# Folds, casts and sums moved off GpSimd in an inference step of a Fourier and latent-attention layer

## The chip, the cores and the metric

One core of a Trainium2 chip runs the kernel. The metric is device time in microseconds of one execution, as the median of several runs. The engines are TensorE (PE, with PEld for its weight loads), VectorE (DVE), ScalarE (ACT), GpSimd (POOL) and SyncE (SP), which issues most DMAs. The profile gives TensorE's granted clock as a fraction of 2.4 GHz; its two levels are 1.2 and 2.4 GHz.

## The reference

One trunk layer over 1024 latent tokens and 128 context tokens of width 1024 (1152 rows, written NT):

```
h      = rms_norm(x) * (1 + scale) + shift          # shift, scale, gate from silu(cond) @ w_ada
u_f, z_f, cq, ckv, k_rope, z_a, g_f, g_a = split(h @ w_in)
y_f    = (Re FFT2(u_f, positions x 128 channels) * silu(z_f)) @ w_f_out
attn   = softmax(q k) v      # 8 heads, low-rank q and kv, latents read 128 cached context rows too
y_a    = (attn * silu(z_a)) @ w_a_out
merged = sigmoid(g_f) * y_f + sigmoid(g_a) * y_a
y      = rms_norm(x + gate * (merged @ w_out)) * final_norm_g
```

Outputs are y for context and latent tokens, and the context's normalised ckv and k_rope.

## The kernel before, in words

All products are made in a rounded 32-bit format: an operand is split into a high part (a cast) and a low part (operand minus high part), and `mm3` (lines 122 to 126) issues three matmuls, high-high, low-high or high-low. So each operand costs a cast and a subtraction before TensorE can use it. `hi_pool` casts on GpSimd, `act.copy` on ScalarE, `lo_dve` (line 109) subtracts on VectorE.

The work falls into stages. (1) The first part, up to about 95 us: x is loaded, scaled and transposed by matmuls; for each of eight channel blocks f of 128 channels, `modulate` makes h (1024 latent columns and 128 context columns), `fold` and `fold2` add and subtract mirrored positions for the Fourier transform (sums s1, differences s2, quarter folds q0 and q1, context folds c2 and c3), `fsplit` makes the high and low parts foh and fol, `hsplit` those of h (hTh, hTl), and `mix` multiplies the folded rows with the channel-transformed weights into five PSUM banks. The steps stand in the list SEQ, an order written by hand: x, u, a are loads, Q R S the norm, T t transposes, c C the modulation's rows, m modulate, s fold, h hsplit, f fold2, g fsplit, w weights, X mix. The table ENG names the engine of each elementwise step: a ScalarE, d VectorE, p GpSimd. (2) A first plain block of w_in (`Plain`), the position transform, three low-rank maps (`low_mm`), a second plain block; meanwhile `combine` loads h again from DRAM and forms differences of its quarters. (3) From about 182 to 426 us, eleven pairs of blocks of w_in (`pair`): each pair is made with seven products in the order 1, 6, 2, 7, 5, 4, 3 in place of eight, from sums of quarter blocks. `Blocks.prepare` makes the weights' sums and splits for the next pair while the present one runs; product 1 lands in bank X, ScalarE copies it into a buffer u, and product 2 accumulates into the same bank. (4) The product with w_f_out and the low-rank rows' transposes, to about 500 us; (5) attention, to about 776 us; (6) the merge, to about 825 us: per block m and a third of the columns, `merge_part` multiplies by the gate, adds the Fourier branch, and splits the sum; (7) the output projection and the last norm.

Tiles of 4.6 KB per partition come from one pool of 43 (`U`); a tile is reused when its last reader is done, and the instruction that writes it next waits for that. Each engine works through its instructions in one fixed order. That order is found when the program is built, by a planner that starts from the order of the code and moves instructions by its own costs.

Of the kernel before, what the change touches and what calls it, by code (L numbers as in the profile page):

```python
# [12 lines left out]
AF = mybir.ActivationFunctionType  # L13
ALU = mybir.AluOpType
# [3 lines left out]
P = 128  # L18
# [21 lines left out]
).split()  # L40
GRP = ((8, 0, 1), (2, 3), (4, 5), (6, 7))
ENG = dict(c0="a", c1="a", c2="d", c3="p", s0="a", s1="d", s2="p", q0="p", q1="d", h0="a", l0="p", h1="a", l1="d", hh="a", hl="d", ma="a", mb="d", mc="d", md="a", ta="d", tb="a", tc="a", wh="a", ar="a")
SCE = "ddddddddd"


# [18 lines left out]
def kernel(ctx: ExitStack, tc: tile.TileContext, a: dict):  # L64
    nc = tc.nc
    pe, act, dve, pool = nc.tensor, nc.scalar, nc.vector, nc.gpsimd
# [19 lines left out]
    def U(shape, dt=F32, s="u"):  # L86
        return upool.tile(shape, dt, tag="u", name=nm(s))
# [4 lines left out]
    def S(shape, dt=F32, tag="s1k", bufs=3, s="s"):  # L92
        return spool.tile(shape, dt, tag=tag, bufs=bufs, name=nm(s))
# [7 lines left out]
    def MM(tag="mm"):  # L101
        tag = tag if tag in banks else "mm"
        return psum.tile([P, 512], F32, tag=tag, bufs=banks[tag], name=nm(tag))

    def hi_pool(out, x):
        pool.tensor_scalar(out=out, in0=x, scalar1=1.0, scalar2=1.0, op0=ALU.mult, op1=ALU.mult)  # L106

    def lo_dve(out, x, hi):
        dve.tensor_tensor(out=out, in0=x, in1=hi.bitcast(F32), op=ALU.subtract)  # L109
# [11 lines left out]
    def mm3(out, lh, ll, rh, rl, start, stop, after=False, on=False):  # L121
        i = pe.matmul(out, lh, rh, start=start, stop=False, skip_group_check=on)  # L122
        if after:
            tc.keep_in_program_order(i)
        pe.matmul(out, lh, rl, start=False, stop=False, skip_group_check=on)  # L125
        pe.matmul(out, ll, rh, start=False, stop=stop, skip_group_check=on)  # L126
# [47 lines left out]
    def load_x(t):  # L174
        x = U([P, D], s="x")
        src = a["x_sample"][t * P : (t + 1) * P, :] if t < 8 else a["x_prompt"]
        nc.sync.dma_start(x, src)
        return x
# [29 lines left out]
    def EQ(k, out, x):  # L208
        e = ENG[k]
        if e == "a":  # L210
            act.copy(out, x)
        elif e == "p":
            hi_pool(out, x)
        else:
            dve.tensor_copy(out, x)

    def TT(k, out, x, y, op):
        (pool if ENG[k] == "p" else dve).tensor_tensor(out=out, in0=x, in1=y, op=op)

# [8 lines left out]
    def ada_rows(parts, kper, n, ps):  # L228
# [10 lines left out]
        ada = S([P, n], tag="s1k", bufs=3) if n == 256 else U([P, n], s="ada")  # L239
        (act.copy if n == 512 or ENG['ar'] == 'a' else dve.tensor_copy)(ada, ps[:, 0:n])  # L240
        return ada
# [4 lines left out]
    def wprime(k):  # L246
# [9 lines left out]
        h = WPh[k // 2][:, k % 2, :].rearrange("p (c g) -> p c g", g=4)  # L256
        (act.copy if ENG["wh"] == "a" else dve.tensor_copy)(h, ps)
        lo_dve(WPl[k // 2][:, k % 2, :].rearrange("p (c g) -> p c g", g=4), ps, h)
# [22 lines left out]
    def modulate(f):  # L281
        hf = hfs[f] = U([P, NT], F32, "hf")
        if f < ND:
            pa, pb = xT.pop(f)
            src = ((0, hf[:, 0:512], pa, ENG["ma"] == "a"), (0, hf[:, 512:NL], pb, ENG["mb"] == "a"), (1, hf[:, NL:NT], xTc[:, f, :], ENG["mc"] == "a"))
        else:
            src = ((0, hf[:, 0:NL], xT.pop(f), ENG["md"] == "a"), (1, hf[:, NL:NT], xTc[:, f, :], ENG["mc"] == "a"))
        for m, out, x, e in src:
# [6 lines left out]
    def fold(f):  # L295
        hf = hfs[f]

        sd = U([P, 2, 513], F32, "sd")
        EQ("s0", sd[:, 0, 0:513:512], hf[:, 0:513:512])
        TT("s1", sd[:, 0, 1:512], hf[:, 1:512], hf[:, 1023:512:-1], ALU.add)  # L300
        TT("s2", sd[:, 1, 1:512], hf[:, 1:512], hf[:, 1023:512:-1], ALU.subtract)
        pool.tensor_scalar(out=sd[:, 1, 0:513:512], in0=sd[:, 1, 256:257].to_broadcast([P, 2]), scalar1=0.5, scalar2=1.0, op0=ALU.mult, op1=ALU.mult)

        fo = fos[f] = U([P, 1153], F32, "fo")
        EQ("c0", fo[:, 1024:1025], sd[:, 0, 256:257])
        EQ("c1", fo[:, 1025:1090:64], hf[:, 1024:1089:64])
        TT("c2", fo[:, 1026:1089], hf[:, 1025:1088], hf[:, 1151:1088:-1], ALU.add)
        TT("c3", fo[:, 1090:1153], hf[:, 1025:1088], hf[:, 1151:1088:-1], ALU.subtract)
        sds[f] = sd
# [236 lines left out]
    def combine(f):  # L546
        xa, xb = U([P, NT], F32, "xa"), U([P, NT], F32, "xb")
        nc.sync.dma_start(xa, h_d[f])
        nc.sync.dma_start(xb, h_d[f + 4])
        x11, x12, x21, x22 = xa[:, lo_half], xa[:, hi_half], xb[:, lo_half], xb[:, hi_half]  # L550
        dve.tensor_tensor(out=x11, in0=x12, in1=x11, op=ALU.subtract)
        pool.tensor_tensor(out=x12, in0=x22, in1=x12, op=ALU.subtract)
        dve.tensor_tensor(out=x22, in0=x22, in1=x11, op=ALU.subtract)
        dve.tensor_tensor(out=x21, in0=x21, in1=x22, op=ALU.subtract)
        h, l = U([P, NT], F32R, "th"), U([P, NT], F32R, "tl")
        act.copy(h, xb)
        lo_dve(l, xb, h)
        t42.append((h, l))
        if f % 2 == 0:
            t33.append((U([P, NT], F32R, "th"), U([P, NT], F32R, "tl")))  # L560
        sl = hi_half if f % 2 else lo_half
        h, l = (x[:, sl] for x in t33[f // 2])
        act.copy(h, x12)
        lo_dve(l, x12, h)
        ones.append(x11)
# [130 lines left out]
    class Blocks:  # L696
# [10 lines left out]
        def prepare(self, j):  # L707
            (a11, a12), (a21, a22) = [(r[:, 0], r[:, 1]) for r in self.raw]
            if j == 6:
                self.s12 = U([P, 2, 512], F32, "ws")  # L710
                pool.tensor_tensor(out=self.s12[:, 0], in0=a21, in1=a22, op=ALU.add)
                pool.tensor_tensor(out=self.s12[:, 1], in0=self.s12[:, 0], in1=a11, op=ALU.subtract)
            elif j == 7:
                self.s34 = U([P, 2, 512], F32, "ws")
                pool.tensor_tensor(out=self.s34[:, 0], in0=a11, in1=a21, op=ALU.subtract)
            elif j == 3:
                pool.tensor_tensor(out=self.s34[:, 1], in0=a12, in1=self.s12[:, 1], op=ALU.subtract)
            x = {1: lambda: a11, 2: lambda: a12, 3: lambda: self.s34[:, 1], 4: lambda: a22, 5: lambda: self.s12[:, 0],
                 6: lambda: self.s12[:, 1], 7: lambda: self.s34[:, 0]}[j]()
            w = U([P, 2, 512], F32R, "wp")  # L720
            hi_pool(w[:, 0], x)
            lo_dve(w[:, 1], x, w[:, 0])
            self.w[j] = w

# [89 lines left out]
    for p in range(2):  # L814
        fourier_out(p)
    combine(0)
    low_out(0, pss)
    pss = low_mm(1)
    combine(1)
    low_out(1, pss)  # L820
    pss = low_mm(2)
    combine(2)
    low_out(2, pss)
    pss = None
# [169 lines left out]
    def q_chunk(wq, c):  # L994
        sl = slice(c * CH, (c + 1) * CH)
        ps = MM()
        for k in range(2):
            ws = slice(k * P, (k + 1) * P)
            mm3(ps[:, :CH], wq[:, 0, ws], wq[:, 1, ws], cqh[k][:, sl], cql[k][:, sl], k == 0, k == 1)
        qf = H([P, CH], s="qf")  # L1000
        dve.tensor_tensor(out=qf, in0=ps[:, :CH], in1=TAB[:, sl], op=ALU.mult)  # L1001
        q = U([P, 2, CH], F32R, "q")
        hi_pool(q[:, 0, :], qf)
        lo_pool(q[:, 1, :], qf, q[:, 0, :])
        return q
# [18 lines left out]
    for m in range(8):  # L1024
# [10 lines left out]
        mf = U([P, NT], F32, "mf")  # L1035
        for c in range(3):
            sl = slice(c * CH, (c + 1) * CH)
# [177 lines left out]
    for h in range(NH):  # L1215
# [3 lines left out]
        q0 = None  # L1219
        for part in LSEQ if h == NH - 1 else HSEQ:  # L1220
# [46 lines left out]
            elif o == "Q":  # L1267
# [3 lines left out]
                elif h + 1 < NH:  # L1271
                    q0 = q_chunk(wq1, 0)
# [12 lines left out]
    def merge_part(m, c):  # L1285
        w, ga, mf = wao[m]
        sl = slice(c * CH, (c + 1) * CH)
        ps = MM()
        for k in range(4):
            mm3(ps[:, :CH], w[:, 0, k, :], w[:, 1, k, :], ath[k][:, sl], atl[k][:, sl], k == 0, k == 3)  # L1290
        dve.tensor_tensor(out=ga[:, sl], in0=ps[:, :CH], in1=ga[:, sl], op=ALU.mult)
        pool.tensor_tensor(out=mf[:, sl], in0=mf[:, sl], in1=ga[:, sl], op=ALU.add)  # L1292
        act.copy(mh[m][:, sl], mf[:, sl])
        lo_dve(ml[m][:, sl], mf[:, sl], mh[m][:, sl])

# [13 lines left out]
    for m, c in ((0, 0), (0, 1), (1, 0), (1, 1), (0, 2), (1, 2)):  # L1309
        merge_part(m, c)  # L1310
    load_out(0)
    load_out(1)
    for m in range(2, 8):
        merge_open(m)
        for c in range(3):
            merge_part(m, c)
        load_out(m)
# [7 lines left out]
    for t in range(9):  # L1325
        x = load_x(t)
        g = gate[0 if t < 8 else 1]
        sl = slice(t * P, (t + 1) * P)
# [4 lines left out]
        for i, (c0, c1) in enumerate(zip(cuts, cuts[1:])):  # L1333
            ps = MM()
            hf, n = c0 // 512, c1 - c0
            for k in range(8):
                wh, wl = wo[hf, k // 2]
# [168 lines left out]
```

## Time and profile before

| quantity | value |
|---|---|
| median of 3 runs | 935.27 us (933.52 to 939.51) |
| the profiled execution: its time, its span | 937.2 us, 935.4 us |
| busy: PE, PEld, DVE, ACT, POOL | 898.3, 849.3, 620.7, 424.2, 404.8 us |
| mean granted clock | 0.990 |
| first matmul of the first plain block | 94.81 us |
| DMA | 115.61 MB, mean 124 GB/s |

The span runs from the first to the last instruction. A busy engine may still be slow, since matmuls' ends are modelled and overlap; the share of an average hides stages with different limits, so the windows are read stage by stage.

### The profile page before, as it was taken

The numbers are of one execution on the slowest core, as the hardware profiler recorded it, in microseconds if no ns is written. First come the engines' busy times: TensorE is split into PE (matmuls) and PEld (weight loads), VectorE is DVE, ScalarE is ACT, GpSimd is POOL, SyncE is SP. The second block draws the span as 40 slices with busy tenths as digits, with TensorE's granted clock in tenths as the row PEclk, the third lists the DMA queues.
The fourth block names the chain that finished last, engine by engine and source line by source line (L and its number), as shares of the span: only waits on it lengthen the run. The fifth ranks groups of instructions, "written<-read, shape, count | busy, mean of one in ns | idle before, by whom it ended". The sixth has DMA issues, their size and how long they took to land.

```text
span 935.4 us, 15960 instructions
## 1 busy us (share of the span) xinstructions
PE 898.3 (96%) x5886; PEld 849.3 (91%) x5886; DVE 620.7 (66%) x1257; ACT 424.2 (45%) x1171; POOL 404.8 (43%) x491
## 2 busy tenths in 40 slices
PE   4988999999999999999999999999999999999996
PEld 3878999999999999988899999999999989988885
DVE  2789456664555545648538889889889888884333
ACT  6555365411122111135227787787787782212111
POOL 0378313574444448932151264264263126863221
PEclk9988999999999999999999999999999999999998
DMA  9733745422223244287743000000000147342222
GB/s 363 313 140 104 230 140 204 159 96 97 96 96 97 96 147 146 96 280 290 264 149 136 6 7 5 7 7 4 7 7 1 63 152 296 122 158 90 90 92 89
DMA packets 35798, 115.61 MB, mean 124 GB/s; under 512 B 4484, under 2 KB 9348, under 8 KB 35720
## 3 DMA queue, kind: packets, MB, share of 16 engines
q1 hardware_dynamic: 31688, 105.94, 31.5%
q10 hardware_dynamic: 3168, 6.16, 1.8%
q0 software_dynamic: 864, 2.49, 0.8%
q8 instruction: 47, 0.77, 0.3%
q14 instruction: 31, 0.25, 0.1%
HBM read 81.74 MB, written 32.83 MB: 122 GB/s over the span
## 4 chain that ended last, share of the span: by engine, by line
PE 75%; POOL 5%; DVE 3%; DMA 3%; ACT 1%; issue 1%; DVEq 0%; SPq 0%; ACTq 0%; POOLq 0%
PE mm L122 20%; PE mm L126 20%; PE mm L125 20%; PE mm L1128 6%; PE mm L1149 4%; PE mm L1148 3%; POOL z L758 1%; POOL wp L106 1%; DMA za_d<-z 1%; POOL z L762 1%; DMA fz_d<-z 1%; DVE tl L109 1%; DMA wr<-in_w_f_out 1%; POOL mfl L1292 1%; DVE hTl L109 0%
## 5 line engine op out<-in xcount | busy, mean ns | idle before, releaser
L1096 DVE TENSOR_REDUCE s<-mm 128x1 f32<-128x384 f32 (+1 forms) x200 | 104.7, 540 | 15.6 <-PE mm L126 13.8
L109 DVE TENSOR_TENSOR tl<-mm,th 128x384 fp32r<-128x384 f32 (+1 forms) x216 | 102.9, 505 | 16.7 <-ACT th L1129 16.1
L1107 ACT ACTIVATE p<-mm,s 128x384 f32<-128x384 f32 x192 | 110.1, 588 | 7.1 <-DVE s L1101 6.8
L122 PE MATMUL mm<-hTh,wp 128*128 128x288 f32 x352 | 103.8, 296 | 1.9 <-ACT u L789 1.9
L125 PE MATMUL mm<-hTl,wp 128*128 128x288 f32 x352 | 103.7, 295 | 0.0
L126 PE MATMUL mm<-hTh,wp 128*128 128x288 f32 x352 | 103.7, 295 | 0.0
L1129 ACT CAST th<-mm 128x384 fp32r<-128x384 f32 (+1 forms) x216 | 89.5, 461 | 25.4 <-PE mm L1128 22.4
L1128 PE MATMUL mm<-c,p 128*128 128x128 f32 x576 | 95.5, 273 | 1.6 <-DVE tl L109 0.5
L1128 PEld LDWEIGHTS mm<-c,p 128*128 128x128 f32 x576 | 71.6, 140 | 8.4 <-DVE tl L109 1.4
L125 PE MATMUL mm<-tl,wp 128*128 128x288 f32 x264 | 77.8, 295 | 1.4 <-DVE tl L109 1.4
L122 PE MATMUL mm<-th,wp 128*128 128x288 f32 x264 | 78.1, 297 | 0.2 <-DVE u L795 0.2
L126 PE MATMUL mm<-th,wp 128*128 128x288 f32 x264 | 77.9, 295 | 0.0
L1149 PE MATMUL mm<-tl,v 128*128 128x384 f32 (+1 forms) x216 | 73.9, 346 | 0.2 <-DVE tl L109 0.2
L1148 PE MATMUL mm<-th,v 128*128 128x384 f32 (+1 forms) x216 | 73.3, 343 | 0.0
L122 PE MATMUL mm<-kh,q 128*128 128x384 f32 x192 | 70.8, 368 | 0.7 <-DVE osb L1162 0.4
L122 PEld LDWEIGHTS mm<-hTh,wp 128*128 128x128 f32 x352 | 66.2, 188 | 2.1 <-ACT u L789 2.1
L125 PEld LDWEIGHTS mm<-hTl,wp 128*128 128x128 f32 x352 | 66.2, 188 | 0.0
L126 PEld LDWEIGHTS mm<-hTh,wp 128*128 128x128 f32 x352 | 66.2, 188 | 0.0
L125 PE MATMUL mm<-kl,q 128*128 128x384 f32 x192 | 64.7, 337 | 0.0
L126 PE MATMUL mm<-kh,q 128*128 128x384 f32 x192 | 63.8, 337 | 0.0
L106 POOL TENSOR_SCALAR q<-qf 128x384 fp32r<-128x384 f32 x24 | 12.3, 512 | 105.5 <-DVE qf L1001 77.7
L122 PE MATMUL mm<-hi,mh 128*128 128x512 f32 (+1 forms) x152 | 57.5, 382 | 0.0
(341 smaller groups left out, 2581.6 us busy)
## 6 DMA issues: line engine op xcount, KB each, us to landing
wr<-in_w_in SPq DMA_DIRECT2D x24, 512.0 KB, 4.1
x<-in_x_sample SPq DMA_DIRECT2D x16, 512.0 KB, 4.9
wada<-in_w_ada SPq DMA_DIRECT2D x16, 512.0 KB, 10.2
h_d<-hf SPq DMA_DIRECT2D x8, 576.0 KB, 3.0
gf_d<-z SPq DMA_DIRECT2D x8, 576.0 KB, 4.3
gfl<-gf_d SPq DMA_DIRECT2D x8, 576.0 KB, 5.1
mf_d<-mf SPq DMA_DIRECT2D x8, 576.0 KB, 3.6
gal<-ga_d SPq DMA_DIRECT2D x8, 576.0 KB, 3.7
```

Source lines behind the costliest of these rows:

```text
L106: pool.tensor_scalar(out=out, in0=x, scalar1=1.0, scalar2=1.0, op0=ALU.mult, op1=ALU.mult)
L109: dve.tensor_tensor(out=out, in0=x, in1=hi.bitcast(F32), op=ALU.subtract)
L122: i = pe.matmul(out, lh, rh, start=start, stop=False, skip_group_check=on)
L125: pe.matmul(out, lh, rl, start=False, stop=False, skip_group_check=on)
L126: pe.matmul(out, ll, rh, start=False, stop=stop, skip_group_check=on)
L758: pool.tensor_tensor(out=out, in0=out, in1=tmp, op=ALU.mult)
L1096: dve.tensor_reduce(out=self.nb if self.last else self.mx[:, kc : kc + 1], in_=ps[:, 0:n], axis=AX.X, op=ALU.min)
L1107: act.activation(self.p[:, kc * CH : kc * CH + n], self.ps[kc][:, 0:n], AF.Exp, scale=-1.0, bias=self.nb, accum_out=SSP[(self.h // 2) % 2] ...
L1128: pe.transpose(pt[:, j * P : (j + 1) * P], self.pr[j][:, kt * P : (kt + 1) * P], ident)
L1129: act.copy(th[:, i, 0:n], pt[:, 0:n])
L1148: pe.matmul(po[:, 0:n], V[kt][:, h, :], th[:, i, 0:n], start=(self.nv == 0), stop=False)
L1149: pe.matmul(po[:, 0:n], V[kt][:, h, :], tl[:, i, 0:n], start=False, stop=(self.nv == 8))
```

## The change

Eight steps change their engine; nothing else does. In the table ENG: the context's difference c3, the difference fold s2, the quarter folds q0 and the second low part l0 go from GpSimd to VectorE; the context's modulation mc and the copies ta of the transposes' first half go from VectorE to ScalarE. In `fold`, the scaling of two columns goes from GpSimd to ScalarE. In `combine`, one of four subtractions goes from GpSimd to VectorE; in `Blocks.prepare` the cast of each weight operand from GpSimd to ScalarE (its sums stay on GpSimd); in `merge_part` the addition from GpSimd to VectorE.

```diff
-ENG = dict(... c3="p", s0="a", s1="d", s2="p", q0="p", q1="d", h0="a", l0="p", ... mc="d", md="a", ta="d", ...)
+ENG = dict(... c3="d", s0="a", s1="d", s2="d", q0="d", q1="d", h0="a", l0="d", ... mc="a", md="a", ta="a", ...)
...
-        pool.tensor_scalar(out=sd[:, 1, 0:513:512], in0=sd[:, 1, 256:257].to_broadcast([P, 2]), scalar1=0.5, scalar2=1.0, op0=ALU.mult, op1=ALU.mult)
+        act.activation(sd[:, 1, 0:513:512], sd[:, 1, 256:257].to_broadcast([P, 2]), AF.Copy, scale=0.5)
...
-        pool.tensor_tensor(out=x12, in0=x22, in1=x12, op=ALU.subtract)
+        dve.tensor_tensor(out=x12, in0=x22, in1=x12, op=ALU.subtract)
...
-            hi_pool(w[:, 0], x)
+            act.copy(w[:, 0], x)
             lo_dve(w[:, 1], x, w[:, 0])
...
-        pool.tensor_tensor(out=mf[:, sl], in0=mf[:, sl], in1=ga[:, sl], op=ALU.add)
+        dve.tensor_tensor(out=mf[:, sl], in0=mf[:, sl], in1=ga[:, sl], op=ALU.add)
         act.copy(mh[m][:, sl], mf[:, sl])
```

## Rows read from the trace of the kernel before

**Rows 1.** Windows: stretch, its length, busy PE PEld DVE ACT POOL (instructions), clock, DMA.

```profile
40.00:96.00 56.00, 48.41 (x363) 43.55 (x360) 49.21 (x61) 32.26 (x59) 41.18 (x42) 0.88 0.35 120
...
182.00:402.00 220.00, 219.79 (x1657) 219.45 (x1656) 119.23 (x179) 41.37 (x97) 132.94 (x142) 1.00 0.30 107
...
776.00:840.00 64.00, 63.19 (x345) 60.59 (x345) 53.52 (x65) 12.70 (x25) 46.78 (x41) 1.00 0.51 184
...
60.00:68.00 8.00, 7.27 (x43) 6.30 (x41) 6.23 (x11) 5.28 (x10) 5.53 (x6) 0.57 0.25 101
```

**Rows 2.** Waits from 36 to 100 us: sum in us, times, longest.

```profile
ACT fo L211 <- DVE sd L218: 12.9, 7, 3.6
ACT fo L211 <- DVE hf L293: 5.9, 3, 3.4
...
PE mm L126 <- DVE fol L218: 2.5, 3, 1.1
```

**Rows 3.** VectorE's groups from 40 to 96 us: count, busy us, mean ns, idle before.

```profile
L218 DVE TENSOR_TENSOR fol<-fo,foh 128x641 fp32r<-128x641 f32 x8 | 13.1, 1647 | 2.3 <-ACT foh L211 2.3
L218 DVE TENSOR_TENSOR hTl<-hf,hTh 128x1152 fp32r<-128x1152 f32 x8 | 11.7, 1471 | 2.4 <-ACT hTh L211 2.3
L218 DVE TENSOR_TENSOR fo<-sd 128x512 f32<-128x512 f32 x7 | 9.1, 1303 | 1.2 <-POOL fo L218 1.2
L218 DVE TENSOR_TENSOR sd<-hf 128x511 f32<-128x511 f32 x6 | 4.5, 744 | 0.0
L293 DVE TENSOR_SCALAR hf<-xTc,c 128x128 f32<-128x128 f32 x6 | 4.3, 732 | 0.0
L109 DVE TENSOR_TENSOR wpl<-mm,wph 128x512 fp32r<-128x512 f32 x5 | 3.3, 684 | 1.5 <-ACT wph L257 1.5
L218 DVE TENSOR_TENSOR fo<-hf 128x63 f32<-128x63 f32 x6 | 2.3, 381 | 0.0
```

**Rows 4.** VectorE's time line where GpSimd is quiet: start, duration.

```profile
65.24 0.81 DVE L218 TENSOR_TENSOR fol<-fo,foh 128x641 fp32r<-128x641 f32 x1
...
66.14 0.21 DVE L218 TENSOR_TENSOR fo<-hf 128x63 f32<-128x63 f32 x1
66.28 0.68 DVE L218 TENSOR_TENSOR sd<-hf 128x511 f32<-128x511 f32 x1
...
87.61 1.34 DVE L218 TENSOR_TENSOR hTl<-hf,hTh 128x1152 fp32r<-128x1152 f32 x1
```

**Rows 5.** GpSimd's largest group from 40 to 92 us.

```profile
L218 POOL TENSOR_TENSOR fol<-fo,foh 128x512 fp32r<-128x512 f32 x8 | 12.3, 1548 | 3.4 <-ACT foh L211 3.3
```

**Rows 6.** ScalarE's cast of 512 columns, from 40 to 96 us.

```profile
L211 ACT CAST foh<-fo 128x512 fp32r<-128x512 f32 x7 | 4.3, 619 | 1.3 <-DVE fo L218 1.3
```

**Rows 7.** TensorE's time line at the start of the paired blocks.

```profile
181.23 0.40 PE L125 MATMUL mm<-tl,wp 128*128 128x288 f32 x1 [1.44 <-DVE tl L109]
```

**Rows 8.** GpSimd's casts and two of its sums, 182 to 402 us.

```profile
L106 POOL TENSOR_SCALAR wp<-ws 128x512 fp32r<-128x512 f32 x40 | 27.3, 683 | 17.2 <-PE mm L126 15.6 <-DVE wp L109 0.6
...
L717 POOL TENSOR_TENSOR ws<-wr,ws 128x512 f32<-128x512 f32 x10 | 17.0, 1701 | 0.0
...
L715 POOL TENSOR_TENSOR ws<-wr,wr 128x512 f32<-128x512 f32 x10 | 13.8, 1384 | 7.1 <-PE mm L126 6.5 <-DVE wp L109 0.6
```

**Rows 9.** Time lines of GpSimd, ScalarE and TensorE at the last pair's start.

```profile
399.91 2.02 POOL L758 TENSOR_TENSOR z<-z,u 128x288 f32<-128x288 f32 x2
...
399.92 0.45 ACT L756 ACTIVATE u<-z 128x288 f32<-128x288 f32 x1 [1.36 <-DVE z L775]
...
412.08 0.40 PE L122 MATMUL mm<-hTh,wp 128*128 128x288 f32 x1 [1.88 <-ACT u L789]
```

**Rows 10.** The merge, 762 to 840 us: two groups, then VectorE's time line.

```profile
L109 DVE TENSOR_TENSOR ml<-mfl,mh 128x384 fp32r<-128x384 f32 x24 | 20.1, 861 | 1.0 <-ACT mh L1293 1.0
...
L1292 POOL TENSOR_TENSOR mfl<-mfl,gal 128x384 f32<-128x384 f32 x24 | 29.8, 1255 | 13.5 <-DVE gal L1291 13.5
...
826.37 1.48 DVE L109 TENSOR_TENSOR ml<-mfl,mh 128x384 fp32r<-128x384 f32 x3
```

More of the change, by code (lines that the diff above doesn't have):

```diff
@@ L41 @@
 GRP = ((8, 0, 1), (2, 3), (4, 5), (6, 7))
-ENG = dict(c0="a", c1="a", c2="d", c3="p", s0="a", s1="d", s2="p", q0="p", q1="d", h0="a", l0="p", h1="a", l1="d", hh="a", hl="d", ma="a", mb="d", mc="d", md="a", ta="d", tb="a", tc="a", wh="a", ar="a")
+ENG = dict(c0="a", c1="a", c2="d", c3="d", s0="a", s1="d", s2="d", q0="d", q1="d", h0="a", l0="d", h1="a", l1="d", hh="a", hl="d", ma="a", mb="d", mc="a", md="a", ta="a", tb="a", tc="a", wh="a", ar="a")
 SCE = "ddddddddd"
```

## The prediction

> **What bounds the kernel now.** I read the table of windows first. TensorE is busy 219.8 of 220 us in the long stage of the paired blocks and 63.2 of 64 us in the merge, but only 48.4 of 56 us between 40 and 96 us, where the folds feed the mixing products; there VectorE is busy 49.2 us and GpSimd 41.2 us [rows 1]. In 60 to 68 us the granted clock is 0.57 on average, between the levels 1.2 and 2.4 GHz: some 6.9 of these 8 us at the lower one. A twin follows at 84 to 92 us. So the 56 us hold up to 7.6 us of idle TensorE, and at the full clock twice 3.4 us more.
>
> Who holds TensorE there is seen in the waits: it waits for VectorE's low parts of the folds, and ScalarE, which casts the high parts, waits 12.9 us for VectorE's first fold and 5.9 us for VectorE's context modulation [rows 2]. VectorE is thus the common cause, busy 88% of the window. The groups of its instructions say why it is so full: a low part of 641 columns costs 1.65 us on average, a quarter fold of 512 columns 1.30 us, a context modulation of only 128 columns 0.73 us [rows 3]. The time line has the same instructions with GpSimd quiet: 641 columns in 0.81 us, 511 in 0.68 us, 63 in 0.21 us, 1152 in 1.34 us; and the one that starts at 66.14 for 0.21 us has its successor start at 66.28, so back to back some 0.07 us of each lies under the next [rows 4]. VectorE pays up to twice its own price because GpSimd works at the same time; GpSimd pays too, 1.55 us for 512 columns [rows 5].
>
> **The change, part by part.** First part, 40 to 96 us. Per channel block f, GpSimd loses the difference fold s2, the context difference c3, the quarter fold q0 and the low part l0; their counts are those of their twins on VectorE: 6, 6, 6 or 7, and 8 [rows 3]. VectorE loses six context modulations, 4.3 us as measured. At the quiet prices it then holds: low parts 8 x 0.81 = 6.5 and 8 x 0.68 = 5.4; hTl 8 x 1.34 = 10.7; quarter folds 13 x 0.68 = 8.8; first folds 12 x 0.68 = 8.2; context folds 12 x 0.21 = 2.5; the weights' low parts 3.3 and some 3.6 of groups too small to show. That is 49 us in 61 - 7 + 26 = 80 instructions, less 80 x 0.07 = 5.6 of overlap: 43.4 us, against 49.2 now. With the 6.8 us of idle that it has today the window comes to 50 us: **6 us saved**. Both ends: 0 if VectorE was not the pace, 12.6 if its idle time goes too. Before 40 us VectorE has idle time for the same additions; I take nothing there.
>
> ScalarE gets per block one cast-like context modulation of 128 columns and a two-column scaling (each between nothing and the 0.62 us of a 512-column cast) and, for some blocks, a 512-column copy at about 0.62 us [rows 6]. With 32.3 us busy of 56 [rows 1] it has room. The scaling adds a wait: it reads the middle of s2, which now follows s1 on VectorE, so ScalarE stands up to 0.68 us longer per block; queued behind it are the cast of hTh, the next modulation and the high parts foh, for which TensorE waits. Against that stand the 5.9 us that it no longer waits for VectorE's modulation. I cost the pair at nothing; if the cover were gone it is 6 x 0.68 = 4 us.
>
> The combination of h before the paired blocks: four subtractions of 576 columns go to VectorE (about 0.76 us each, an estimate by columns from 0.68 us for 512). There TensorE stands 1.44 us behind VectorE's low part tl [rows 7]. The first block's casts leave GpSimd just ahead of it, so VectorE's queue moves faster. I take **1.4 us** saved; ends: 0.8 us lost, by one subtraction more in that queue, and 1.4 gained.
>
> The paired blocks: 77 casts of 512 columns, 0.68 us each on GpSimd, go to ScalarE at 0.62 us [rows 6, 8]; 7 x 0.62 = 4.3 us per pair of 22 us (seven products, below), where ScalarE is busy 41.4 of 220 us [rows 1]. TensorE has no idle time there to give. At the end it stands 1.88 us behind a ScalarE copy whose buffer is still being stored; that store waited for GpSimd's product until 401.93 us, while its sigmoid ended at 400.37 us [rows 9]. GpSimd without casts would finish at about 400.4 + 1.0 (one of the row's two products): **0.5 us** saved; ends 0 and 1.9.
>
> The merge: 24 additions of 384 columns, 1.26 us each on GpSimd, go to VectorE at 1.48 / 3 = 0.49 us: 11.8 us more. Its low parts ml now cost 0.86 us beside GpSimd, 0.49 us alone: 24 x 0.37 = 8.9 us, of which I take 7 back, as GpSimd keeps its casts [rows 10]. VectorE goes from 53.5 to about 58 of 64 us, still under TensorE's 63.2 [rows 1]. I cost this at **0**; ends: 0.8 us gained (TensorE's idle time there) and, if nothing comes back, 53.5 + 24 x 0.86 = 74 us, 10 us lost.
>
> Sum against the profiled execution, 937.2 us (a span of 935.4 and 1.8 around it): 6 + 1.4 + 0.5 = 7.9 us less, 929.3 us. That execution lies 1.9 us above the median of the runs, 935.3 us, so on that scale I forecast **927 us**.
>
> Here the Trainium skill is divided. Perfetto Trace Analysis, section Optimizing Scalar/DVE Operations, says that where VectorE is saturated, handing work to ScalarE or even GpSimd may make sense; VectorE at 88% is such a case, and the change hands work back. SBUF, State Buffer, section Who interferes with whom, says that a VectorE instruction with two inputs in SBUF and a GpSimd instruction that reads SBUF exclude each other. The trace agrees with the second where it shows 1.65 us beside 0.81 us for one form. By the first alone the result would be the third rival below.
>
> **The rivals.** First, the window opens wholly: once VectorE is down to 43.4 us nothing else holds TensorE, the clock stays at 2.4 GHz, and the window shrinks to VectorE's time, 12.6 us less; with 1.4, 1.9 and 0.8 that is 16.7 us, 918.6 us. For it speaks that both slow stretches of the clock lie inside this window; against it that ScalarE and VectorE hand each block to and fro, so that some idle time belongs to the chain.
>
> Second, the gain is hidden: the folds' chain through ScalarE, or a changed order of the instructions (the planner orders them by its own costs, and the new engines change what it sees), sets the pace, and only 0 to 3 us come back: 934 us. For it: TensorE's waits with a VectorE name sum to only a few us [rows 2]; against it VectorE's 88%.
>
> Third, slower: VectorE becomes the bound of the first part. If the prices stay as they are beside GpSimd, the 26 moved instructions cost 8 x 1.3 (1.65 by columns), 6 x 0.74, 6 x 1.30 and 6 x 0.38, together 25 us; 49.2 - 4.3 + 25 = 70 us, with the old idle time 77 us in place of 56: 21 us more, less 2 elsewhere, 954 us. It decides from a mean of 49.2 / 80 = 0.62 us per instruction; at the quiet prices it is 0.54. Against it: GpSimd has nothing else to do between 40 and 90 us.
>
> Fourth, slower by a wait that moves: ScalarE's casts of the next pair's sums now stand in one queue with the copy that TensorE needs before product 2 writes into the same bank. That copy has 1.5 products' time, 4.8 us (a product is 24 of the 1657 matmuls in 220 us, 3.2 us [rows 1]). GpSimd's four sums take 1.4 to 1.7 us each [rows 8], some 6.0 us; if all of them stood ahead of the cast ahead of the copy, 6.0 + 0.6 - 4.8 = 1.8 us would be lost at each of ten pairs, 18 us, less 8 elsewhere: 945 us. It decides where the sums end more than 4 us after the previous pair. Against it: casts are made a pair ahead, and GpSimd gets faster.
>
> **How the numbers follow.** Forecast 0.54 (own range 922 to 932), open window 0.16, hidden 0.20, VectorE bound 0.04, ScalarE's queue 0.06. From 918 to 937 us some 0.8 lies: below it half of the open case's tail, above it both slow cases and a little of the hidden one. One per cent, about what a measurement of this kernel can tell from no change, is 9.4 us: faster means below 925.9 us. The forecast lies just short of that; I give 0.24 of its 0.54 to faster, and all of the open case: 0.40. Slower than 944.6 us: 0.08. The rest, 0.52, is within.
>
> **What would show it.** In the changed profile the low part of 641 columns should cost about 0.8 us, VectorE should be busy some 43 us from 40 us to the start of the first plain block, and that block should start near 89 us (now 94.8 us, in the table above); ScalarE's wait for the context modulation should be gone, and one for s2 new. At the paired blocks' start and end the 1.44 and 1.88 us should shrink; in the merge VectorE should reach about 58 us with ml near 0.6 us. The forecast is wrong if the first plain block starts at 93 us or later with VectorE idle, if TensorE shows waits for ScalarE's copies u at the pairs, or if the merge ends with TensorE waiting for VectorE.

## The result and the profile after

The changed kernel takes 921.99 us (median; 921.18 to 923.01), the kernel before 935.09 us beside it: a ratio of 0.9854 [0.9827, 0.9881], 1.5% faster. The forecast was 927.0 us, the range 918 to 937. The profiled execution after has a span of 920.1 us against 935.4; of these 15.3 us, 1.9 are the profiled execution of before lying above its median. The change is ten moves: six entries of the table ENG and four lines of code (the description above says eight).

I followed the gain through the stages by the first matmul of each: the first plain block starts at 84.42 us, 10.4 earlier; the first matmul of the pairs at 162.9 in place of 173.7 (the description above has about 182), 10.8 earlier; from the first to the last of the pairs' matmuls on the latents' h it takes 244.5 in place of 249.6 us, another 5.1; the output projection starts at 806.8 in place of 822.5, 15.7 earlier; the span ends 15.3 earlier. So the first part brought two thirds, the pairs one third, and attention, the merge and the end nothing. A part of the 10.4 us, at most 2.5, lies in the profiled execution of before and not in the change; the run with the rest alone, below, shows it.

The windows: first before, from 40 us to the first plain block, then after, the same columns as [rows 1]; the third of after is the merge from its first matmuls on:

```profile
40.00:94.80 54.80, 47.22 (x356) 42.35 (x353) 48.73 (x61) 32.26 (x59) 39.98 (x38) 0.88 0.34 120
```

```profile
40.00:84.40 44.40, 41.03 (x350) 37.85 (x349) 42.24 (x72) 33.60 (x70) 6.35 (x14) 0.96 0.44 157
172.00:386.00 214.00, 214.00 (x1617) 214.00 (x1616) 103.68 (x174) 78.95 (x166) 85.51 (x72) 1.00 0.31 112
760.00:824.00 64.00, 62.85 (x345) 60.44 (x344) 55.58 (x89) 12.77 (x25) 17.70 (x17) 1.00 0.52 176
...
76.00:80.00 4.00, 4.00 (x23) 3.78 (x22) 4.00 (x5) 4.00 (x6) 4.00 (x6) 0.62 0.23 66
```

From 40 us to the first plain block VectorE was busy 48.73 of 54.8 us before; now it is 42.24 of 44.4. Its idle time went from 6.1 to 2.2 us. Two stretches at the lower clock, some 6.9 us each, have become one of some 3.4 us, most of it at 76 to 80 us. GpSimd has 6.35 us of work in these 44.4 us, 39.98 before.

VectorE's groups of after from 40 to 82 us answer to [rows 3] (count, busy us, mean ns, idle before):

```profile
L218 DVE TENSOR_TENSOR hTl<-hf,hTh 128x1152 fp32r<-128x1152 f32 x7 | 9.5, 1353 | 1.1 <-ACT hTh L211 1.0
L218 DVE TENSOR_TENSOR fo<-sd 128x512 f32<-128x512 f32 x12 | 8.3, 692 | 0.9 <-ACT sd L302 0.3
L218 DVE TENSOR_TENSOR sd<-hf 128x511 f32<-128x511 f32 x12 | 8.2, 686 | 0.0
L218 DVE TENSOR_TENSOR fol<-fo,foh 128x641 fp32r<-128x641 f32 x7 | 6.5, 941 | 0.0
...
L218 DVE TENSOR_TENSOR fo<-hf 128x63 f32<-128x63 f32 x12 | 2.1, 219 | 0.0
```

About twice as many folds, each at the price of [rows 4]. The 641-column low part is at 0.94 us on average, since one of the seven runs beside GpSimd's first weight cast and takes 1.67 us; every other one takes 0.82 us.

The waits of after from 36 to 84 us (sum, times, longest), for [rows 2]:

```profile
ACT sd L302 <- DVE sd L218: 3.2, 3, 1.8
PE mm L122 <- ACT foh L211: 3.1, 2, 2.5
ACT fo L211 <- DVE sd L218: 2.7, 5, 0.7
```

ScalarE waited 12.9 us for VectorE's first fold and 5.9 us for its modulation; the second wait is gone, the first is 2.7 us, and the new one for s2, behind which the scaling stands, is 3.2. What TensorE still waits for here is a high part foh, 2.49 us at 75.70 us, just ahead of the low clock:

```profile
75.70 0.48 PE L122 MATMUL mm<-wph,foh 128*66 128x260 f32 x1 [2.49 <-ACT foh L211]
```

The pairs: ScalarE's casts from 172 to 386 us, and one of GpSimd's sums there:

```profile
L721 ACT CAST wp<-ws 128x512 fp32r<-128x512 f32 x40 | 24.8, 620 | 39.4 <-PE mm L126 15.4 <-POOL ws L712 11.3 <-POOL ws L717 7.5
```

```profile
L717 POOL TENSOR_TENSOR ws<-wr,ws 128x512 f32<-128x512 f32 x10 | 17.1, 1708 | 0.0
```

The cast costs 0.62 us as taken from [rows 6], the sums cost what they did in [rows 8], and TensorE shows neither the 1.44 nor the 1.88 us [rows 7, 9]. The chain that ended last lost GpSimd's share, 5% before:

```profile
PE 81%; DVE 3%; ACT 2%; DMA 1%; issue 0%; POOL 0%; DVEq 0%; ACTq 0%; SPq 0%; POOLq 0%
```

### The profile page after: what moved, and what is told of

The parts are those of the page before. It is cut to its first block, busy times and chain, and to the rows that moved or that the text cites. A ratio compares the mean times of both kernels' runs of the same rounds, so it can differ in the third digit from the quotient of the medians.

```text
span 920.1 us, 15887 instructions
## 1 busy us (share of the span) xinstructions
PE 888.8 (97%) x5886; PEld 844.5 (92%) x5886; DVE 603.6 (66%) x1304; ACT 472.6 (51%) x1269; POOL 273.4 (30%) x346
## 3 DMA queue, kind: packets, MB, share of 16 engines
q0 software_dynamic: 864, 2.49, 0.8%
## 4 chain that ended last, share of the span: by engine, by line
PE 81%; DVE 3%; ACT 2%; DMA 1%; issue 0%; POOL 0%; DVEq 0%; ACTq 0%; SPq 0%; POOLq 0%
PE mm L122 23%; PE mm L126 22%; PE mm L125 22%; PE mm L1128 6%; PE mm L1149 3%; PE mm L1148 3%; DVE tl L109 1%; DMA wr<-in_w_f_out 1%; DVE lo L109 0%; DVE s L1096 0%; ACT p L1107 0%; ACT th L1129 0%; PE mm L1183 0%; DVE whl L109 0%; PE mm L913 0%
## 5 line engine op out<-in xcount | busy, mean ns | idle before, releaser
L125 PEld LDWEIGHTS mm<-hTl,wp 128*128 128x128 f32 x352 | 66.2, 188 | 0.0
L122 PEld LDWEIGHTS mm<-hTh,wp 128*128 128x128 f32 x352 | 66.2, 188 | 0.0
L126 PEld LDWEIGHTS mm<-hTh,wp 128*128 128x128 f32 x352 | 66.2, 188 | 0.0
L711 POOL TENSOR_TENSOR ws<-wr 128x512 f32<-128x512 f32 x11 | 15.1, 1372 | 150.1 <-DVE z L775 51.2
L775 DVE TENSOR_TENSOR z<-mm,u 128x288 f32<-128x288 f32 x66 | 29.8, 455 | 43.2 <-PE mm L126 43.1
```

The lines of the kernel that those rows point to most:

```text
L775: dve.tensor_tensor(out=outs[i][:, sl], in0=ps, in1=t, op=ALU.add)
```

## The experiments

**First part alone** (the table ENG and the scaling as after, the rest as before).

```diff
+ENG = dict(... c3="d", ... s2="d", q0="d", ... l0="d", ... mc="a", ta="a", ...)
+        act.activation(sd[:, 1, 0:513:512], sd[:, 1, 256:257].to_broadcast([P, 2]), AF.Copy, scale=0.5)
         # combine, prepare, merge_part as before
```

> Only the first part of the change (the table ENG and the two-column scaling); casts, combination and merge as before. Theory: all of the first part's 10.4 us comes from here, so the first plain block starts near 84.4 us and the time is 925 us; the stalls of 1.44 and 1.88 us at the paired blocks remain. Rival: the first part's gain needs GpSimd free of its later work too (its queue runs ahead), then the block starts later than 87 us and the time is 928 us or more.

929.88 us against 935.79, 0.9937 [0.9918, 0.9956]. The first plain block starts at 83.66 us, 11.2 earlier, so the first part keeps all it has in the whole change. But the pairs take 252.3 us, 2.7 more than before, and the time misses the 925 us of the theory, though the block starts where it said. TensorE's time line at their start:

```profile
170.58 0.61 PE L125 MATMUL mm<-tl,wp 128*128 128x288 f32 x1 [1.87 <-DVE tl L109]
```

and the windows around it:

```profile
168.00:172.00 4.00, 2.13 (x10) 1.90 (x11) 3.59 (x5) 0.47 (x2) 1.89 (x3) 0.76 0.74 246
172.00:176.00 4.00, 4.00 (x27) 4.00 (x27) 4.00 (x5) 0.41 (x1) 2.77 (x3) 0.81 0.06 23
```

The 1.44 us of [rows 7] became 1.87, and the clock then stands at 0.76 and 0.81 on average, some 3.4 us at the lower level, 1.7 us lost. TensorE comes to the combination of h 11 us earlier, and VectorE, which works there beside GpSimd's sums and casts, isn't ready; that the early arrival is the reason is argued, since the order of VectorE's work there is another one too (below). The stall at the pairs' end is 2.1 us. The gain of the first part is real, and part of it is taken back one stage later.

**The rest alone** (the first part as before).

```diff
 ENG and the scaling as before
+        dve.tensor_tensor(out=x12, in0=x22, in1=x12, op=ALU.subtract)
+            act.copy(w[:, 0], x)
+        dve.tensor_tensor(out=mf[:, sl], in0=mf[:, sl], in1=ga[:, sl], op=ALU.add)
```

> The change without its first part: casts on ScalarE, one subtraction and the merge's sum on VectorE. Theory: the paired blocks take 5 us less, the merge is unchanged, 930 us. Rival: the paired blocks gained only because everything reached them earlier (loads and stores then meet other traffic); then 934 us or more.

931.03 us, 0.9950 [0.9935, 0.9966]. The pairs take 244.7 us, 5.0 less than before, without either stall. In medians the two halves bring 5.9 and 4.8 us, together 10.7, and the whole change 13.1: the missing 2.4 are about what the first half gives back at the pairs when it is alone.

This run also tells how much of the first part's 10.4 us is the change. Its first part has the instructions of before in the same order on every engine, and yet the first plain block starts at 92.29 us in place of 94.81:

```profile
40.00:92.30 52.30, 43.69 (x352) 38.01 (x351) 46.22 (x60) 31.72 (x58) 37.48 (x35) 0.97 0.34 119
```

```profile
94.82 0.44 PE L126 MATMUL mm<-hTh,lo 128*128 128x384 f32 x1 [1.32 <-DVE lo L109]
```

Here one stretch of some 3.4 us is at the lower clock, where the profiled execution of before had two of 6.9 us. Half of the lead is lost again in a wait for VectorE's low part of the block's weights, and at the pairs 0.9 us of it are left (172.8 against 173.7 us). So 0.9 to 2.5 us belong to the profiled execution of before. Against this run the whole change brings the plain block 7.9 us forward, and the two medians, which differ by the first part alone, lie 9.0 us apart.

**Casts back on GpSimd** (the rest as after).

```diff
-            act.copy(w[:, 0], x)
+            hi_pool(w[:, 0], x)
```

> The changed kernel with the 77 casts back on GpSimd. Theory: the casts carry the gain of the paired blocks; TensorE's stalls there come back in part, 925 to 927 us. Rival: the subtraction of the combination carries it; then 922 to 923 us.

926.80 us, 0.9906 [0.9880, 0.9932]; the pairs take 249.3 us, as before the change. Both stalls are back, in the waits from 150 to 195 and from 395 to 425 us:

```profile
PE mm L125 <- DVE tl L109: 0.9, 1, 0.9
```

```profile
PE mm L122 <- ACT u L789: 2.0, 1, 2.0
```

The casts carry the whole gain of the pairs.

**Subtraction back on GpSimd** (the rest as after).

```diff
-        dve.tensor_tensor(out=x12, in0=x22, in1=x12, op=ALU.subtract)
+        pool.tensor_tensor(out=x12, in0=x22, in1=x12, op=ALU.subtract)
```

> The changed kernel with the combination's subtraction back on GpSimd. Theory: nothing is lost, since GpSimd no longer has the casts queued there: 922 us. Rival: the 1.44 us stall comes back: 923.5 us.

921.57 us, 0.9851 [0.9831, 0.9871], the pairs 244.6 us: with the casts on ScalarE the subtraction's engine is worth nothing. With the casts on GpSimd it may be worth 3 us: the first part alone (252.3 us, stall 1.87 and a low clock) and the kernel with the casts back (249.3 us, stall 0.9 and the clock at 1.00 throughout) differ ahead of the merge in this step and in the order that the planner then made of VectorE's work there (with the first part alone some low parts tl stand behind later blocks' small steps); the two are not separated.

**GpSimd reads SBUF beside the folds** (after, with 14 additions of 128 columns per channel block into a buffer that nothing else uses).

```diff
         sds[f] = sd
+        for _ in range(14):
+            pool.tensor_tensor(out=scr, in0=ident, in1=mods[:, f, 0, 0:1].to_broadcast([P, P]), op=ALU.add)
...
+    scr = C([P, P], F32, "scr")
```

> The changed kernel, with 14 additions of 128 columns per channel block added on GpSimd in the first part; they read two operands in SBUF, write a scratch tile that nobody reads, and nothing waits for them. Theory (VectorE pays for GpSimd's reads): VectorE's folds of 512 columns rise from 0.69 us to over 1 us, the first part grows from 44.4 us by 4 us or more, 926 to 932 us. Rival (what counts is that the blocks no longer pass through GpSimd's queue): prices and time stay, 922 us.

945.25 us, 1.0112 [1.0097, 1.0127]. VectorE's groups from 40 to 82 us:

```profile
L218 DVE TENSOR_TENSOR sd<-hf 128x511 f32<-128x511 f32 x12 | 9.9, 822 | 0.0
L218 DVE TENSOR_TENSOR fo<-sd 128x512 f32<-128x512 f32 x12 | 8.8, 731 | 0.7
```

The prices rise, 686 to 822 and 692 to 731 ns, less than the 1 us that I expected, and the last group of mixing products starts at 90.7 us in place of 84.1. But most of the loss is a mishap of the experiment: the dose was too high, and the first plain block's weight cast stood behind the additions in GpSimd's queue:

```profile
PE mm L122 <- POOL hi L106: 15.1, 1, 15.1
```

So the time proves nothing here; the prices and the end of the products count.

**GpSimd writes SBUF beside the folds** (one such addition and 26 fills of the same buffer per block).

```diff
         sds[f] = sd
+        pool.tensor_tensor(out=scr, in0=ident, in1=mods[:, f, 0, 0:1].to_broadcast([P, P]), op=ALU.add)
+        for _ in range(26):
+            pool.memset(scr, 0.0)
...
+    scr = C([P, P], F32, "scr")
```

> The same, with one addition and 26 fills of 128 columns per block on GpSimd, which only write. Theory: if it is the reading that collides, VectorE's folds stay at 0.7 us and the time at 922 us. Rival: any GpSimd work at the same time costs VectorE; then as in the run with additions.

923.33 us, 0.9882 [0.9865, 0.9898]. GpSimd's fills from 36 to 110 us, and VectorE's groups from 40 to 82 us:

```profile
L312 POOL MEMSET scr<- 128x128 f32 x175 | 36.0, 206 | 10.0
```

```profile
L218 DVE TENSOR_TENSOR fo<-sd 128x512 f32<-128x512 f32 x12 | 8.3, 691 | 0.9 <-ACT sd L302 0.3
L218 DVE TENSOR_TENSOR sd<-hf 128x511 f32<-128x511 f32 x12 | 8.2, 685 | 0.0
```

36 us of GpSimd work, beside every one of these folds, and VectorE's prices are those of after; the last group of products starts at 84.0. The 1.3 us lost are again the weight cast, 1.31 us late behind the fills. It is GpSimd's reading of SBUF that makes VectorE's folds dear, not its being busy. The Trainium skill, SBUF — State Buffer, section Who interferes with whom, says so: a VectorE instruction with two SBUF inputs contends with a GpSimd instruction that reads SBUF, not with one that only writes it. 822 and 685 ns for one instruction in the two runs agree.

**Wide reads** (four additions of 352 columns and one of 63 on the block's h, off the chain).

```diff
         sds[f] = sd
+        for n in (352, 352, 352, 352, 63):
+            pool.tensor_tensor(out=scr[:, 0:n], in0=hf[:, 0:n], in1=hf[:, 512 : 512 + n], op=ALU.add)
...
+    scr = C([P, 352], F32, "scr")
```

> The changed kernel, with four additions of 352 columns and one of 63 per channel block added on GpSimd in the first part: about the GpSimd work that the change took away, but nobody waits for it. Theory (VectorE pays for the length of the GpSimd instruction that holds the shared access): VectorE's folds of 512 columns rise to 0.9 us or more, the mixing products end at 89 us or later (84.1 without the additions), time 926 us or more. Rival (the hand-offs were the cost): prices stay near 0.7 us, the products end at 85 us, 922 us.

942.87 us, 1.0085 [1.0062, 1.0108]. The first plain block starts at 106.23 us, straight after the last group of mixing products (from 105.9): this time the folds are the loss, with no cast standing in GpSimd's queue ahead of TensorE. VectorE's quarter folds from 40 to 82 us, then the time line of GpSimd and VectorE:

```profile
L218 DVE TENSOR_TENSOR fo<-sd 128x512 f32<-128x512 f32 x10 | 9.8, 978 | 0.6
```

```profile
47.95 11.82 POOL L311 TENSOR_TENSOR scr<-hf 128x352 f32<-128x352 f32 x10 [4.35 <-DVE s L278]
...
50.32 0.68 DVE L218 TENSOR_TENSOR sd<-hf 128x511 f32<-128x511 f32 x1
...
54.35 1.43 DVE L218 TENSOR_TENSOR sd<-hf 128x511 f32<-128x511 f32 x1
...
56.71 1.54 DVE L218 TENSOR_TENSOR fol<-fo,foh 128x641 fp32r<-128x641 f32 x1
58.18 1.42 DVE L218 TENSOR_TENSOR sd<-hf 128x511 f32<-128x511 f32 x1
```

and the window from 40 us to the block's start:

```profile
40.00:106.20 66.20, 49.39 (x369) 42.60 (x369) 64.42 (x82) 37.39 (x76) 43.33 (x48) 0.87 0.33 115
```

The quarter fold costs 0.98 us where after has 0.69. VectorE's 511-column folds take 0.68 to 0.69 or 1.41 to 1.44 us (two of fourteen lie between) and their mean is 1.17 from 36 to 92 us; nearly all either go at once or take 0.75 us more, a good part of one of GpSimd's additions (1.18 us each, back to back). VectorE is busy 64.4 of 66.2 us and is the bound. Some 40 us of reading by GpSimd that nobody needs, about as much GpSimd time as in the run with fills, made the first plain block 21.8 us later, about what the third rival had put for a first part bound by VectorE (21).

**Only the folds moved** (before, with c3, s2, q0 and l0 on VectorE).

```diff
-ENG = dict(... c3="p", s2="p", q0="p", l0="p", ...)
+ENG = dict(... c3="d", s2="d", q0="d", l0="d", ...)
```

> The kernel before, with only the four folds and low parts of the first part moved to VectorE; context modulation, copies and the two-column scaling stay where they were. Theory: VectorE's prices fall to the quiet ones at once; the first plain block starts at 86 to 88 us (84.4 with the whole change), and the time is 930 to 932 us, as with the first part alone. Rival: ScalarE's wait for the context modulation is the cause; then the block starts at 92 us or later, 934 us or more.

934.36 us, 0.9990 [0.9977, 1.0003]: no gain, which I had not foreseen. In the first part it is there: VectorE's fold takes 0.69 us and the plain block starts at 86.37 us, 8.4 earlier than before and 5.9 earlier than with the rest alone. The pairs then take 254.2 us, 4.6 more than before. At their start:

```profile
174.92 0.85 PE L122 MATMUL mm<-th,wp 128*128 128x288 f32 x2 [4.03 <-ACT th L556]
```

```profile
176.00:180.00 4.00, 3.69 (x15) 3.69 (x16) 3.59 (x7) 0.00 (x0) 3.19 (x3) 0.50 0.01 4
```

After that the clock is 0.50 from 176 to 180 us. Four us are waited for the high part th, which waits for the combination's VectorE work. The planner also made another order for that work here (the four low parts hTl stand ahead of the next block's subtractions), so the early arrival and the order are not separated in this run.

**Only the modulation and the copies moved** (before, with mc and ta on ScalarE).

```diff
-ENG = dict(... mc="d", ... ta="d", ...)
+ENG = dict(... mc="a", ... ta="a", ...)
```

> The kernel before, with only the context modulation and the copies of the transposes moved from VectorE to ScalarE; all folds as before. Theory: VectorE keeps its dear prices and loses 5 us of work; the plain block starts at 90 to 93 us, 932 to 934 us. Rival: ScalarE's wait is the cause; the block starts at 87 us or earlier, 929 us or less.

940.96 us, 1.0068 [1.0049, 1.0086]: slower, against my expectation. The plain block starts at 91.57 us, 3.2 earlier than before but only 0.7 earlier than with the rest alone; VectorE's quarter fold stays at 1.60 us, since GpSimd still folds. The pairs take 257.8 us, 8.1 more, after a wait of 4.85 us for th, again with the combination in another order. So a part of a change that makes the whole faster made the kernel slower by itself.

**Modulation and scaling back** (after, with mc and ta on VectorE and the scaling on GpSimd).

```diff
-ENG = dict(... mc="a", ... ta="a", ...)
+ENG = dict(... mc="d", ... ta="d", ...)
-        act.activation(sd[:, 1, 0:513:512], sd[:, 1, 256:257].to_broadcast([P, 2]), AF.Copy, scale=0.5)
+        pool.tensor_scalar(out=sd[:, 1, 0:513:512], in0=sd[:, 1, 256:257].to_broadcast([P, 2]), ...)
```

> The changed kernel with the context modulation and the transposes' copies back on VectorE and the two-column scaling back on GpSimd; the four folds, the casts, the subtraction and the sums stay as changed. Theory: the first plain block starts 2 us later than in the changed kernel, as it did with the folds alone, and the paired blocks keep their gain, so 924 us: the folds alone then showed no gain only because the paired blocks' start gave it back. Rival: the modulation and the copies carry the gain of the first part; 930 us or more.

924.51 us, 0.9891 [0.9867, 0.9915]. The plain block starts at 85.52 us, 1.1 later than after; the pairs take 246.0 us, 1.5 more than after and 3.6 less than before:

```profile
PE mm L125 <- DVE tl L109: 0.8, 1, 0.8
```

The folds and low parts thus carry all but 1.1 us of the first part's gain, and with the casts on ScalarE the pairs keep most of theirs. That also tells how to read the run with only the folds: the missing gain was lost at the pairs.

**Merge additions back on GpSimd** (the rest as after).

```diff
-        dve.tensor_tensor(out=mf[:, sl], in0=mf[:, sl], in1=ga[:, sl], op=ALU.add)
+        pool.tensor_tensor(out=mf[:, sl], in0=mf[:, sl], in1=ga[:, sl], op=ALU.add)
```

> The changed kernel with the merge's 24 additions back on GpSimd. Theory: nothing is gained or lost, since TensorE bounds the merge either way: 922 us. Rival: VectorE is too full in the merge of the changed kernel; then this one is 1 us or more faster.

923.50 us (922.12 to 924.01), 0.9876 [0.9852, 0.9900]; a span of 920.3. The merge is 1.1 us longer than after (48.1 against 47.0 us from the last attention matmuls to the first output projection), of which 0.8 us is a wait for GpSimd's cast of whl. The first part came out 1.2 us shorter. Its instructions and their order are those of after, and so is the wait for foh; but here the clock did not fall behind it:

```profile
74.86 0.34 PE L122 MATMUL mm<-wph,foh 128*66 128x260 f32 x1 [2.49 <-ACT foh L211]
```

```profile
76.00:80.00 4.00, 3.49 (x29) 3.11 (x28) 4.00 (x6) 3.98 (x6) 4.00 (x7) 1.00 0.48 97
```

The medians, of two series, differ by 1.5 us. The three runs that keep the additions on GpSimd with only the first part, the folds, or the modulation moved have a merge of 48.1 us too, but the kernel before, with the same additions on GpSimd, has 46.7. So the additions' engine is worth some 1.1 us in the kernel after, and nothing between before and after. VectorE's groups from 744 to 824 us, first after, then this run:

```profile
L1292 DVE TENSOR_TENSOR mfl<-mfl,gal 128x384 f32<-128x384 f32 x24 | 15.6, 649 | 0.6
L109 DVE TENSOR_TENSOR ml<-mfl,mh 128x384 fp32r<-128x384 f32 x24 | 14.7, 636 | 0.1
```

```profile
L109 DVE TENSOR_TENSOR ml<-mfl,mh 128x384 fp32r<-128x384 f32 x24 | 19.5, 839 | 0.6 <-ACT mh L1293 0.6
L109 DVE TENSOR_TENSOR lo<-wr,hi 128x1024 fp32r<-128x1024 f32 x8 | 13.3, 1666 | 1.3 <-POOL hi L106 1.3
```

**One step later** (after, with the split h3 moved behind h7 in the list SEQ): the last wait of the first part.

```diff
-    "X30 g40 X31 X40 f5 g50 m7 w7 g51 h3 X41 s7 g61 X50 f7 g60 X51 X60 h7 X61 g70 h2 g71 h6 X70 X71 "
+    "X30 g40 X31 X40 f5 g50 m7 w7 g51 X41 s7 g61 X50 f7 g60 X51 X60 h7 h3 X61 g70 h2 g71 h6 X70 X71 "
```

> The changed kernel with one step of the order moved: the split of h for block 3 after that for block 7. In the changed kernel its low part stands ahead of the last block's folds on VectorE while TensorE waits 2.5 us for that block's high parts. Theory: the wait shrinks by 1 to 2 us and the time is 920 to 921 us. Rival: VectorE's total work up to the first plain block bounds it, and the time stays at 922 us.

920.16 us (919.76 to 921.59), 0.9846 [0.9818, 0.9875], a span of 918.4 and a mean clock of 0.999: the fastest of all kernels here, though the intervals of this ratio and of the change's overlap. The wait of 2.49 us went, and with it the low clock behind it; TensorE's time line and the window:

```profile
73.64 0.34 PE L122 MATMUL mm<-wph,foh 128*66 128x260 f32 x1 [0.17 <-ACT foh L211]
```

```profile
76.00:80.00 4.00, 3.13 (x27) 2.92 (x26) 4.00 (x4) 3.98 (x6) 3.94 (x5) 1.00 0.28 88
```

ScalarE's cast hTh (1.15 us) and VectorE's hTl (1.35 us) no longer stand ahead of the second split of block 6 and the folds of block 7; the plain block starts at 82.32 us, 2.1 earlier. Of these 2.1 us, 1.2 also came in the run before this one, which has the wait but not the low clock; and at the pairs both are level (161.75 and 161.70 us, after 162.91). So what the step brings later on is about the price of the low clock, which it avoids (the mean clock of its four runs is 0.998 or 0.999, after's 0.996).

## Why the prediction was right, and where it was off

**The bound.** VectorE at its dear prices was the bound of the first part; the runs with GpSimd's reads and writes show the cause, and the prices of [rows 4] held to 2% for the folds (692 and 686 ns against 0.68 us). But one reading of those rows was wrong. The low part of 641 columns that starts at 65.24 us did not run with GpSimd quiet:

```profile
65.40 0.83 POOL L218 TENSOR_TENSOR fo<-hf 128x63 f32<-128x63 f32 x1 [0.16 <-DVE hf L293]
```

VectorE had started first and took its own 0.81 us; it was GpSimd's subtraction of 63 columns that took 0.83 us in place of 0.32 (at 37.66 us). The price of 0.81 us was right all the same, as the 0.82 us of after shows; in this pair the one that started first kept its price, and the other paid.

**First part, 6 us forecast, 10.4 measured between the two profiles.** Against the run with the rest alone, which has the same 3.4 us of low clock as after, it is 7.9 us, and 9.0 in medians; so the forecast was 2 to 3 us short. The block, put near 89 us, came at 84.42. VectorE's busy time was sized well: 43 us forecast up to the plain block, 42.2 measured. The term that was mis-sized is "with the 6.8 us of idle that it has today". The idle time up to the plain block fell by 3.9 us too, from 6.1 to 2.2, and it is 6.1 with the rest alone as well. That it was made by the same delays is argued from the waits: ScalarE waited 18.8 us for VectorE [rows 2] and waits 5.9 now, new wait included, so it hands its parts back sooner. What is left against the first rival (12.6 us) is for the most part the one wait of 2.49 us for foh and the clock behind it; the run with h3 later opened another 2.1 us.

**ScalarE's additions at nothing.** About right as a sum in the first part: putting modulation, copies and scaling back costs 1.1 us there. It costs another 1.5 us at the pairs, which the prediction did not have. The wait for s2 came, 3.2 us in three waits of up to 1.8 us, where up to 0.68 us per block was put, and the 5.9 us went.

**The combination and the casts, 1.9 us forecast, 5.1 measured.** The mechanism was right, the size was not. I counted the stall at the start whole (1.4), of the one at the end a quarter (0.5 of 1.88), and no more. These two terms were too small: both stalls went wholly, and more with them. In matmuls, the first 8.3 us of the pairs held 52 before and hold 65 now: at 0.132 us each, from 1617 in 214 us, that is 1.7 us, stall and restart. In the last 22 us before 149 ran where 166 go at this pace, 2.2 us more. The rest is spread thinly. The run with the casts back shows that it is the casts, and the one with the subtraction back that the subtraction adds nothing to them.

**The merge at 0.** Right: it takes 46.7 us before and 47.0 after. VectorE was put at 58 of 64 us and ml near 0.6, and is at 55.6 and 0.64.

**The rivals.** Hidden gain: it is what the folds or the modulation show when moved alone, since the pairs' start took it back; in the whole change the casts on ScalarE and the low prices at the combination (hTl of 576 columns 0.76 us against 1.30 before and 1.44 with the first part alone) prevent it. VectorE as the bound: false, as its prices fell with GpSimd's reads; the wide reads show the size it would have had. The advice that spoke for it, of the Trainium skill, Perfetto Trace Analysis, section Optimizing Scalar/DVE Operations, adds that handing work to and fro between these two engines might not help, which the prediction left out; the folds, which carry nearly all of the first part's gain, bear the addition out. ScalarE's queue at the pairs: no such wait is in the trace, TensorE is busy 214 of 214 us.

**The size.** 922.0 us lies 5 us below the forecast, some 2 to 3 us of it in the first part and 3 at the pairs. It lies 3.9 us below the bound of 925.9 for faster by 1%, on the side to which I gave 0.40, while 0.52 went to no such change. So the mechanism was right and the gain, 13.1 us for 8.3, was under-sized at both places.

What stays open: how much of the pairs' loss in the runs with the first part or one piece of ENG alone is the early arrival and how much the planner's other order; whether the casts held the pairs back by their place in GpSimd's queue or by their reads beside VectorE; and why the merge before is 1.4 us shorter than in the other kernels with the additions on GpSimd.

## What to carry to other kernels

Where VectorE and GpSimd both read SBUF, price a moved instruction by rows in which the other engine is quiet, and expect the idle time that their delays made to shrink with the busy time. A stage that gets faster brings TensorE earlier to the next one: look what it meets there before the gain is booked, and fear above all a stall that is followed by the lower clock. One profile of a kernel is one execution: compare its stages with another run that has the same instructions there. Try parts of a change together as well as alone; here two parts that belong to a gain of 1.5% were worth nothing and minus 0.7% by themselves.

## What the runs showed of the hardware

GpSimd's fills cost VectorE nothing at 36 us of them, its reads cost more the longer they were: additions of 128 columns raised VectorE's 511-column folds from 0.69 to 0.82 us, additions of 352 columns to 1.17 us, with 0.68 or 1.43 us as nearly all of the single values. The context modulation, one tensor with two scalars for each row, is dear beside GpSimd as well: 0.73 us for 128 columns in [rows 3], 0.34 us with the modulation back on VectorE and GpSimd quiet:

```profile
L293 DVE TENSOR_SCALAR hf<-xTc,c 128x128 f32<-128x128 f32 x6 | 2.0, 343 | 0.0
```

And one late operand can cost TensorE twice: 4.03 us waited for th were followed by a clock of 0.50 from 176 to 180 us. It need not: the wait of 2.49 us for foh was followed by some 3.4 us at the lower clock in after, and by none with the merge additions back on GpSimd.
